# A hybrid decoder layer on one core: halo rows, y splits and one projection step change their places around the output projection

## The chip, the cores and the metric

The kernel runs on one core of a Trainium2 chip. A core has a matrix engine (TensorE, PE in the profile; its weight loads are PEld), a vector engine (VectorE, DVE), a scalar engine (ScalarE, ACT), GpSimd (POOL) and a queue engine that here issues every DMA (SyncE, SP). Each engine works off its own list of instructions in order and waits on semaphores of the others. The metric is device time in microseconds of one execution; the kernel before is given as the median of three.

## The reference, cut to what matters

One layer, float32, 16 meta tokens ahead of 1024 tokens, model width 1024:

```python
xn = rms_norm(h, mix_pre_g)
proj = xn @ w_in                       # z, xbc, dt, q, k, v
y_ssd = ssd_mixer(z, xbc, dt, ...)     # 16 heads, chunks of 128
y_sb = rms_norm(stick_breaking_attention(q, k, v), sb_norm_g)
mix = concat([y_ssd, y_sb]) @ w_out    # 2048 -> 1024
h = h + rms_norm(mix, mix_post_g)
xn = rms_norm(h, ffn_pre_g)
gu = xn @ w_up                         # 2 x 2816 columns
g = causal_dwconv(gu[..., :D_FF], ffn_conv_w, ffn_conv_b)   # 3 taps
f = (gelu(g) * gu[..., D_FF:]) @ w_down
h = h + rms_norm(f, ffn_post_g)
return h[:, N_META:]
```

The convolution of three taps makes token t need the tokens t-1 and t-2. So the last two meta tokens are carried through the mixer and the norm as well, though they are not put out: they are the "halo" below, two rows beside the eight blocks of 128 tokens.

## The kernel before, in words

Every float32 product is made of three passes over rounded parts: an operand x is split into a rounded high part (ScalarE, a copy) and a low part x - high (VectorE or GpSimd, a subtraction), and PE adds high·high, high·low and low·high.

**The attention part.** A loop over eight head pairs p and eight query blocks i. A step makes the scores z (L765), two sigmoids per score tile (kp and bt, L766 and L767, ScalarE), a scan (L773, VectorE), a product (L775, GpSimd), and, some steps later, turns the weights bt by PE transposes (tw, L787), copies them out (th, L789) and multiplies with the values (av, L802, copied out at L805). Score tiles and turned tiles share two PSUM buffers of one tag ("zz"), so a transpose waits until an older score tile is read, and a score tile until an older turned tile is copied. Between these, `fill` gives the projections of q, k and v in half chunks (pj_k and the like, L165), and W_out's first half is loaded and split in eight rows (L887 and L888). "Corner turns" (`edge_turn`, twc, L811, then thc, L814) and `edge_mix` (avc, L822) bring in the keys of block borders once per head pair, at i = 2 and i = 3. At (p, i) = (7, 1) the halo of the first half of W_out begins (`halo_rows`, L916: 64 matmuls of two rows in one PSUM tile, copied out in eight small pieces at L923 and stored by SP), and behind it the first output chain `first` (`ssd_half`, mo, L951, copied out as ma, L963). In this part PE's order is that of the program text; the other engines are ordered by a scheduler. The PSUM tag "mm" has two buffers for pj, halo and mo.

**The second output chain.** A loop t = 1 to 8 over blocks of 128 tokens; from t = 2 on PE, VectorE, ScalarE and GpSimd run in the order of the program text (`manual_schedule`), SP's order is the scheduler's. For a block:

- y (the attention's result, from DRAM) is split: yh (L938, ScalarE) and yl (L939, VectorE for t up to 5, GpSimd after). The buffers of yh and yl hold two blocks.
- mo: two halves of 512 columns, 24 matmuls each (L951); each half is added to the stored first part by VectorE (L1436) in one instruction, which frees the PSUM buffer.
- `after`: square and row sum (L1120, ScalarE), root (L191 and L192, GpSimd), scale and add x (L1123 and L1124, VectorE), square again (L1129), root, scale (L1133, giving oxn). The last two stand in the next step.
- `turn_x2`, two steps later: eight PE transposes (x2tp, L1139) and for t up to 4 two rounded copies, two plain copies (L1145 and L1146, ScalarE) and two subtractions (L1147, VectorE).

The halo goes the same way as a thin block of two rows: `halo_sum` (L1199), `after(0, ...)`, and `turn_x2(0, 2, ...)`. A two-row instruction of 1024 columns lasts as long as one of 128 rows. After the loop come the first feed-forward products (g0a, u0a), then the feed-forward stage to the end.

Names with numbers: x2tp0 is the halo's transpose tile and x2tp3 that of block 3; mo1_5_0 is the first column half of block 5 in the second chain; oxn, jk and mb carry the block too.

Of the kernel before, what the change touches and what calls it, by code (L numbers as in the profile page):

```python
# [9 lines left out]
F32 = mybir.dt.float32  # L10
# [7 lines left out]
P = 128  # L18
# [9 lines left out]
NT = T // P  # L28
# [25 lines left out]
def tile_layer(ctx: ExitStack, tc: tile.TileContext, x, meta, rows, parts,  # L54
               w_z, w_xbc, w_dt, w_q, w_k, w_v, w_out, w_up, w_down, out):
    nc = tc.nc
# [113 lines left out]
    def run(steps, n=None):  # L170
        for _ in steps if n is None else zip(range(n), steps):
            pass
# [280 lines left out]
    with tc.tile_pool(name="ssd", bufs=1, side="right") as sp:  # L453
# [135 lines left out]
        fill = flow([x_flow(0, 0), x_flow(0, 1)], 2)  # L589
# [118 lines left out]
        fill = flow(xz_flow(1), 2)  # L708
# [98 lines left out]
    def edge_turn(p):  # L807
        cb = edges.pop(p)
        tw = psum_tp(f"twc{p}")
        for j in range(2):  # L810
            nc.tensor.transpose(tw[:, j, :], cb[:, j].rearrange("p t c -> p (t c)"), ident)  # L811
        th = ap.tile([P, 2, 4, P], F32, tag="th", name=f"thc{p}", bufs=2).rearrange("p h b c -> p h (b c)")
        for j in range(2):
            nc.vector.tensor_tensor(th[:, j, :256].rearrange("p (t c) -> p t c", c=32),  # L814
                                    tw[:, j, 96:P].unsqueeze(1).to_broadcast([P, NT, 32]), cmask, op=ALU.mult)
        return th
# [95 lines left out]
    def halo_rows(pool, half, y0, w, acc):  # L912
        for k in range(8):
            yield
            for c in range(4):
                mm(acc[32 * c:32 * c + 2, :], y0[:, k, :], w[k][c // 2][:, 512 * (c % 2):512 * (c % 2) + 512].bitcast(F32),  # L916
                   start=k == 0, stop=k == 7)
        for a in (0, 256):
            mh = pool.tile([P, 256], F32, tag="ma", name=f"mh{half}_{a}", bufs=1)
            for c in range(4):  # L920
                b = 512 * (c % 2) + a
                rows_ = slice(32 * c, 32 * c + 2)
                nc.scalar.activation(mh[rows_], acc[rows_, a:a + 256], AF.Copy)  # L923
                nc.sync.dma_start(out=halod[2 * half + c // 2][:, b:b + 256], in_=mh[rows_])
# [3 lines left out]
    def load_y(half, t, yk):  # L928
        nc.sync.dma_start(out=yk, in_=yd1[t - 1] if half else yd[t])
        return yk  # L930

    def split_y(pool, half, t, tags, yk=None, eng=nc.gpsimd):
        nm = f"{half}_{t}"
        if yk is None:
            yk = load_y(half, t, yraw[0](f"yk{nm}"))
        yh = pool.tile([P, 8, P], F32R, tag=tags[0], name=f"yh{nm}", bufs=tags[2])
        yl = pool.tile([P, 8, P], F32R, tag=tags[1], name=f"yl{nm}", bufs=tags[2])
        nc.scalar.activation(yh, yk, AF.Copy)  # L938
        eng.tensor_tensor(yl, yk, yh.bitcast(F32), op=ALU.subtract)  # L939
        return yh, yl  # L940
# [48 lines left out]
    for p in range(8):  # L989
        for i in range(NT):  # L990
            if p == 0 and i == 0:
                run(fill, 1)
            block = block_weights(p, i)
            next(block, None)
            if mix:
                block_mix(*mix.pop(0))
            if p > 0 and i == 3:
                edge_mix(p - 1, edge)
            run(fill, 1 + (i < FILL[p]))
            if first:  # L1000
                run(first, 1)
            run(block)
            if (p, i) == (7, 1):
                halo = halo_rows(ap, 0, y0a, wres, psum_mm("halo0"))
                run(halo, 3)
            ahead = iter(())
            if len(turn) > 2:
                ahead = begin_turn()
            if (p, i) == (7, 1):
                run(halo, 2)  # L1010
            if i < NT - 1:
                run(ahead)
            run(fill, int(p > 0 or i > 3))
            if (p, i) == (7, NT - 1):
                run(first, 1)
            run(ahead)
            if left[0] and wsteps is None:
                wres = []
                wsteps = wout_steps(third_slots(), 0, ssd_g, wres, [])
                y0a = halo_y(ap, 0)  # L1020
            if (p, i) == (6, 3):
                yk = [load_y(0, 1, rp.tile([P, L + 3], F32, tag="rq", name="yk0_1", bufs=3)[:, :D]
                             .rearrange("p (a b) -> p a b", b=P)),
                      load_y(0, 2, rp.tile([P, L], F32R, tag="rk", name="yk0_2", bufs=3).bitcast(F32)[:, :D]
                             .rearrange("p (a b) -> p a b", b=P))]
            if left[1] and not ys1:
                ys1.append(split_y(wp, 0, 1, ("whi", "wlo", WB), yk[0], nc.vector))
            for _ in range(2):
                if wsteps and len(wres) < min(8, 3 * left[0], STAGE.get((p, i), 0)):
                    run(wsteps, 1)  # L1030
            if wsteps and first is None and len(wres) == 8:
                run(wsteps)
                first = ssd_half(wres, ys1)
                run(first, 1)
                ys1.append(split_y(wp, 0, 2, ("whi", "wlo", WB), yk[1], nc.vector))
            elif first:
                run(first, 1)
                run(halo)
            if p == 7 and 2 < i < 6:
                run(meta_steps, 1)  # L1040
            if p == 0 and i == 2:
                token_rstd(r_ssd, ap, "a")
            if p > 0 and i == 2:
                edge = edge_turn(p - 1)
    while turn or mix:
        if mix:
            block_mix(*mix.pop(0))
# [3 lines left out]
    edge = edge_turn(7)  # L1051
# [372 lines left out]
    for t in range(1, NT + 1):  # L1424
        if t == 2:
            order.enter_context(tc.manual_schedule(engines=ORDERED))
        if 1 < t < NT - 1:
            yk = load_y(1, t + 1, yraw[0](f"yk1_{t + 1}"))
        if mts:
            mt = mts.pop(0)  # L1430
        else:
            mt = f1.tile([P, 1032], F32, tag="gr", name=f"mb{t}", bufs=2)[:, :D]
            nc.sync.dma_start(out=mt, in_=mixd[t - 1])

        def ev2(acc, cs, mt=mt, t=t):
            nc.vector.scalar_tensor_tensor(mt[:, cs], acc, r_sb[:, t:t + 1], mt[:, cs], op0=ALU.mult, op1=ALU.add)  # L1436

        if t == 5:
            b22s.append(qp.tile([P, 4, 2 * P], F32, name="b22s", tag="b22s"))
        if t < NT:  # L1440
            xt = wp_f32("wlo", f"xr{t}") if t > 2 else wp.tile([P, D], F32, tag="wraw", name=f"xr{t}")
            nc.sync.dma_start(out=xt, in_=x[(t - 1) * P:t * P, :])
        if t == 7:
            xt8 = qp.tile([P, D], F32, name="xr8", tag="xr8")
            nc.sync.dma_start(out=xt8, in_=x[T - P:, :])
            for jj in range(2):
                load_raw(jj, 0, wp, "wraw", 2)
        steps = out_steps(1, t, wres2, ys.pop(0), ev2)
        run(steps, 2)
        run(norm, 1)  # L1450
        if len(pend) > 1:
            turn = pend.pop(0)()
            run(turn, 2)
            run(norm)
            if t == NT:
                run(steps)
            run(turn)
        run(norm)
        if 1 < t < NT - 1:
            ys.append(split_y(op, 1, t + 1, ("yh", "yl", 2), yk, nc.vector if t < 5 else nc.gpsimd))  # L1460
        if t == 2:
            halo_sum(2)
        elif t == 3:
            halo_sum(3)
            halo_norm = after(0, halo_mt, 2, halo_xt, halo_mo, halo_mo)
            run(halo_norm, 1)
        elif t == 4:
            run(halo_norm)
        if t == 7:
            g0.split_1()  # L1470
            load_raw(0, 1, wp, "wraw", 2)
        elif t == NT:
            g0_pair = pair_w("2g0")
            u0.split_1()
            g0.split_2(g0_pair)
            load_raw(1, 1, wp, "wraw", 2)
        run(steps)
        if t == 6:
            edge_x2()
        if t == NT:  # L1480
            break
        if t == 6:
            ys.append(split_y(op, 1, NT, ("yh", "yl", 2)))
        xn = f1.tile([P, 1032], F32, tag="fa", name=f"oxn{t}")[:, :D]
        junk = psum_fa(f"jk{t}").rearrange("p a b -> p (a b)")
        norm = after(t, mt, P, xt, xn, junk)
        run(norm, 1)
        if t == 7:
            xt = xt8
        run(norm, 2)  # L1490
        pend.append(lambda t=t, xn=xn: turn_x2(t, P, xn, x2_tiles(t)))
        if t == 3:
            run(halo_norm, 2)
        elif t == 4:
            run(turn_x2(0, 2, halo_mo, x2_tiles(0)))
    opool.close()
    tA, tB = ExitStack(), ExitStack()
# [372 lines left out]
```

## Time and profile before

| | us |
|---|---|
| median of three runs (lowest, highest) | 1745.74 (1743.22, 1745.97) |
| the profiled execution, whole | 1741.94 |
| its span, first to last instruction | 1740.0 |
| attention steps with the first output chain, up to | about 945 |
| second output chain, from, to | 968, 1075 |
| feed-forward, from, to | 1075, 1740 |

The profile is of one execution, and every time of an instruction is counted from the start of its span. A row of the timeline gives start, length, engine, line, operation, output and inputs, shapes and count; behind it in brackets the idle time of that engine just before, and whose end released it. The view of waits adds up these idle times by the pair of waiting and releasing line. PE's matmuls overlap: one of 512 columns has a length of 0.39 us, but the next starts 0.23 us after it.

### The profile page before, as it was taken

The page shows a single profiled execution, that of the slowest core. Times are in us where ns is not written, and L with a number is a line of the kernel's source. Part 1 is how long each engine was busy: PE and PEld are TensorE (multiplying, and loading weights), DVE is VectorE, ACT ScalarE, POOL GpSimd, SP SyncE. Part 2 cuts the span into 40 slices and gives each one's busy share as a digit, 9 for nine tenths or more (in the row PEclk, how much of TensorE's full clock was granted, in tenths as well). Part 3 has the DMA queues.
Part 4 walks back from the last instruction along what each step waited for, and adds up shares of the span by engine and source line. Part 5 has one row for each costly group of instructions (what it writes and reads, how often), then busy time and mean ns, then how long its engine had stood idle before and what let it go on. Part 6 is the DMA issues. An engine that isn't in the chain of part 4 may idle for free.

```text
span 1740.0 us, 28052 instructions
## 1 busy us (share of the span) xinstructions
PE 1707.8 (98%) x11230; PEld 1496.6 (86%) x11230; DVE 1121.2 (64%) x1230; ACT 822.9 (47%) x1374; POOL 857.9 (49%) x645
## 2 busy tenths in 40 slices
PE   7999999999999999999999979999999999999998
PEld 6999889888999998998687768999988888887886
DVE  5752964775676677668532457676666666658777
ACT  5423653545566566558553234533333333343544
POOL 4323663686565566555552124487776777400001
PEclk9999999999999999999999999999999999999999
DMA  4233343231011011122215443232332222395335
GB/s 163 63 110 98 98 135 109 65 95 38 26 37 45 30 37 32 31 62 73 82 57 199 165 145 122 67 116 97 105 108 91 92 91 91 108 322 199 104 110 181
DMA packets 90694, 173.88 MB, mean 100 GB/s; under 512 B 10714, under 2 KB 35834, under 8 KB 90564
## 3 DMA queue, kind: packets, MB, share of 16 engines
q1 hardware_dynamic: 90564, 172.10, 31.2%
q8 instruction: 88, 1.44, 0.4%
q14 instruction: 42, 0.34, 0.1%
HBM read 122.33 MB, written 49.73 MB: 99 GB/s over the span
## 4 chain that ended last, share of the span: by engine, by line
PE 89%; issue 3%; DVE 3%; ACT 2%; POOL 2%; DMA 1%; POOLq 0%; DVEq 0%; SPq 0%; ACTq 0%
PE fX L1280 10%; PE dnA L1690 7%; PE fY L1280 6%; PE fA L1280 6%; PE mo L951 6%; PE pj_k L165 5%; PE pj_v L165 5%; PE pj_z L165 5%; PE dnB L1690 5%; PE pj_q L165 5%; PE pj_X L165 5%; PE av L802 4%; PE z L765 3%; PE tw L787 3%; PE pj_B L165 1%
## 5 line engine op out<-in xcount | busy, mean ns | idle before, releaser
L775 POOL TENSOR_TENSOR bt<-bt,kp 128x256 f32<-128x256 f32 (+7 forms) x128 | 213.0, 1683 | 185.5 <-DVE kp L773 135.2
L773 DVE TENSOR_TENSOR_SCAN kp<-kp,hold 128x272 f32<-128x272 f32 (+7 forms) x128 | 183.4, 1473 | 25.3 <-ACT kp L766 15.0
L1223 POOL TENSOR_TENSOR wlo<-wr,whi 128x1024 fp32r<-128x1024 f32 x43 | 107.9, 2518 | 38.4 <-ACT whi L1222 38.4
L1727 POOL TENSOR_TENSOR fms<-fms 128x1 f32<-128x1 f32 x8 | 3.2, 394 | 223.4 <-ACT dh L1612 197.0
L766 ACT ACTIVATE kp<-z 128x288 f32<-128x288 f32 (+6 forms) x112 | 82.6, 737 | 50.9 <-PE z L765 27.5
L1222 ACT ACTIVATE whi<-wr 128x1024 fp32r<-128x1024 f32 x43 | 45.6, 1060 | 111.6 <-PE fX L1280 68.3
L165 PE MATMUL pj_v<-xs,wh_v 128*128 128x400 f32 (+2 forms) x384 | 94.9, 334 | 0.0
L1352 DVE SCALAR_TENSOR_TENSOR ga<-gr,pp,ga 128x1024 f32<-128x1024 f32 x44 | 72.3, 1643 | 34.9 <-ACT ga L1345 34.1
L165 PE MATMUL pj_k<-xs,wh_k 128*128 128x400 f32 (+2 forms) x384 | 94.5, 333 | 0.0
L165 PE MATMUL pj_q<-xs,wh_q 128*128 128x386 f32 (+2 forms) x384 | 93.9, 331 | 0.0
L789 ACT ACTIVATE th<-tw 128x1024 f32<-128x1024 f32 (+2 forms) x96 | 75.6, 816 | 38.5 <-PE tw L787 38.4
L1612 ACT ACTIVATE dh<-ar 128x512 fp32r<-128x512 f32 x77 | 48.5, 630 | 92.7 <-PE dnB L1690 44.7
L165 PE MATMUL pj_X<-xs,wh_X 128*128 128x400 f32 (+2 forms) x384 | 92.0, 327 | 0.2 <-ACT craw_X L211 0.2
L165 PE MATMUL pj_z<-xs,wh_z 128*128 128x386 f32 (+2 forms) x384 | 91.5, 326 | 0.0
L951 PE MATMUL mo<-woa,yh 128*128 128x512 f32 x256 | 84.4, 398 | 2.1 <-ACT ma L963 1.2
L1613 DVE TENSOR_TENSOR dl<-ar,dh 128x512 fp32r<-128x512 f32 x77 | 53.2, 692 | 50.4 <-ACT dh L1612 50.3
L741 DVE CAST qh<-q 128x128 fp32r<-128x128 f32 x64 | 45.7, 715 | 59.7 <-PE z L765 59.4
L767 ACT ACTIVATE bt<-z 128x288 f32<-128x288 f32 (+6 forms) x112 | 82.9, 740 | 0.0
L802 PE MATMUL av<-th,v 128*64 128x128 f32 x1152 | 77.2, 278 | 0.0
L787 PE MATMUL tw<-ident,bt 128*128 128x128 f32 x576 | 75.7, 274 | 0.9 <-ACT bt L767 0.5
L802 PEld LDWEIGHTS av<-th,v 128*64 128x64 f32 x1152 | 61.5, 136 | 13.8 <-issue 11.1
L787 PEld LDWEIGHTS tw<-ident,bt 128*128 128x128 f32 x576 | 65.5, 141 | 7.1 <-issue 3.3
(558 smaller groups left out, 5648.8 us busy)
## 6 DMA issues: line engine op xcount, KB each, us to landing
wr<-in_w_up SPq DMA_DIRECT2D x44, 512.0 KB
fds<-ga SPq DMA_DIRECT2D x44, 256.0 KB
b<-in_w_down SPq DMA_DIRECT2D x44, 256.0 KB
ar<-fds SPq DMA_DIRECT2D x44, 256.0 KB
fda<-ga SPq DMA_DIRECT2D x33, 256.0 KB
ar<-fda SPq DMA_DIRECT2D x33, 256.0 KB
yk<-yd SPq DMA_DIRECT2D x16, 512.0 KB
wor<-in_w_out SPq DMA_DIRECT2D x12, 512.0 KB
```

The costliest lines, as they stand in the source:

```text
L165: mm(acc[:ncol, :n - s], a[:, k, :ncol], xs[c0][:, b, k, s:n], start=(k == 0 and j == 0), stop=(k == KB - 1 and j == 2))
L766: nc.scalar.activation(kp[:, :, a:a + w], z[:, :, :w], AF.Sigmoid, scale=-QSCALE)
L767: nc.scalar.activation(bt[:, :, a:a + w], z[:, :, :w], AF.Sigmoid, scale=QSCALE)
L773: nc.vector.tensor_tensor_scan(kp[:, j][:, ::-1], kp[:, j][:, ::-1], hold[:, L - n:L][:, ::-1], 0.0, op0=ALU.mult, op1=ALU.max)
L775: nc.gpsimd.tensor_tensor(bt[:, j, 0:m], bt[:, j, 0:m], kp[:, j, 1:m + 1], op=ALU.mult)
L787: nc.tensor.transpose(tw[:, j, b, :], bt[:, j, c0:c0 + P], ident)
L789: nc.scalar.activation(th[:, :, :nb, :], tw[:, :, :nb, :], AF.Copy)
L802: mm(av[halves[j], :], v[:, kb, halves[j]], th[:, j, b, :], start=kb == 0, stop=kb == i)
L951: mm(acc, u[:, k, :], v[:, cs], start=(k == 0 and j == 0), stop=(k == 7 and j == 2))
L1223: nc.gpsimd.tensor_tensor(l, raw, h.bitcast(F32), op=ALU.subtract)
L1280: mm(acc[:, c, :nn], u[:, k, :], v[:, k, c0:c0 + nn], start=first and k == 0 and j == 0, stop=k == 3 and j == 2, skip_group_check=not first)
L1690: mm(banks[BANK[n], t], u[:, 0, c], v[:, 1, :], start=(n in (1, 2, 5) and p == 0 and i == 0), stop=(p == NPR - 1 and i == 2), skip_group_c ...
```

## The change

```diff
         for a in (0, 256):
-            mh = pool.tile([P, 256], F32, tag="ma", name=f"mh{half}_{a}", bufs=1)
+            mh = pool.tile([P, 256], F32, tag="ma", name=f"mh{half}_{a}", bufs=2)
...
             ahead = iter(())
+            if (p, i) == (6, 6):
+                run(fill, 1)
             if len(turn) > 2:
                 ahead = begin_turn()
...
-            run(fill, int(p > 0 or i > 3))
+            run(fill, int((p > 0 or i > 3) and (p, i) != (6, 6)))
...
+            if p > 0 and i == 2:
+                edge = edge_turn(p - 1)
             for _ in range(2):
                 if wsteps and len(wres) < min(8, 3 * left[0], STAGE.get((p, i), 0)):
                     run(wsteps, 1)
...
             elif first:
+                run(halo)
                 run(first, 1)
-                run(halo)
...
-            if p > 0 and i == 2:
-                edge = edge_turn(p - 1)
...
-        if 1 < t < NT - 1:
-            yk = load_y(1, t + 1, yraw[0](f"yk1_{t + 1}"))
+        if t == 1:
+            yk = load_y(1, 3, yraw[0]("yk1_3"))
...
         run(steps, 2)
         run(norm, 1)
+        if 1 < t < NT - 1:
+            ys.append(split_y(op, 1, t + 1, ("yh", "yl", 2), yk, nc.vector if t < 5 else nc.gpsimd))
+            yk = load_y(1, t + 2, yraw[0](f"yk1_{t + 2}"))
         if len(pend) > 1:
...
         run(norm)
-        if 1 < t < NT - 1:
-            ys.append(split_y(op, 1, t + 1, ("yh", "yl", 2), yk, nc.vector if t < 5 else nc.gpsimd))
...
         if t == 6:
-            ys.append(split_y(op, 1, NT, ("yh", "yl", 2)))
+            ys.append(split_y(op, 1, NT, ("yh", "yl", 2), yk))
...
-        elif t == 4:
+        elif t == 5:
             run(turn_x2(0, 2, halo_mo, x2_tiles(0)))
```

It does five things. The small halo copies get a second buffer. At step (6, 6) of the attention the second half of a projection chunk goes ahead of a turn. The corner turn goes ahead of W_out's rows in the text of a step, and at (7, 2) the rest of the halo's matmuls ahead of the next piece of the first output chain. In the second chain each y block is split in the middle of a step, ahead of the turn, and loaded a step earlier. And the halo's own transposes go from the end of step 4 to the end of step 5.

Three places show how instructions move. First ScalarE at step (6, 6) (th6_4 are the copies of the turned tiles tw6_4, kh7 the copy of the projection pj_k7, yh0_2 a split of a y block of the first chain, ysc a copy of av, kp6_7 the first sigmoid on the next score tile). Before:

```order
L805 ACTIVATE ysc6_8441<-av6_3_8675 128x128
L789 ACTIVATE th6_4_0_8707<-tw6_4_0_8698 128x1024
L789 ACTIVATE th6_4_1_8712<-tw6_4_1_8709 128x2x128
L938 ACTIVATE yh0_2_9002<-yk0_2_8487 128x1024
L388 ACTIVATE kh7_8088<-pj_k7_784_8685 128x256
L766 ACTIVATE kp6_7_8736<-z6_7_0_8738 128x2x348
```

In the changed kernel:

```order
L805 ACTIVATE ysc6_8441<-av6_3_8675 128x128
L938 ACTIVATE yh0_2_9002<-yk0_2_8487 128x1024
L388 ACTIVATE kh7_8088<-pj_k7_784_8685 128x256
L789 ACTIVATE th6_4_0_8721<-tw6_4_0_8712 128x1024
L789 ACTIVATE th6_4_1_8726<-tw6_4_1_8723 128x2x128
L766 ACTIVATE kp6_7_8736<-z6_7_0_8738 128x2x348
```

The two copies of the turned tiles went behind the y split and the projection's copy, as on PE the ten transposes tw6_4 went behind the twelve matmuls of pj_k7 and now stand directly ahead of the score tile z6_7_0.

Second PE at step (7, 2) (mo0_1_0 and mo0_1_1 are the column halves of block 1 in the first chain, twc6 the corner turn of head pair 6). Before:

```order
L951 MATMUL mo0_1_1_9079<-woa400_8643,yl0_1_8729 128x512
L951 MATMUL mo0_1_1_9079<-woa400_8643,yh0_1_8728 128x512
L916 MATMUL halo0_8945<-woa400_8643,y00_8396 2x512 x8
L916 MATMUL halo0_8945<-woa784_8906,y00_8396 2x512 x8
L811 MATMUL twc6_9126<-ident_69,cb6_8109 128x128 x2
L765 MATMUL z7_3_0_9134<-kh7_8088,qh7_3_9017 128x264 x2
```

In the changed kernel:

```order
L951 MATMUL mo0_1_0_8989<-woa784_8906,yh0_1_8728 128x512
L787 MATMUL tw7_0_0_9074<-ident_69,bt7_0_8837 128x128 x2
L811 MATMUL twc6_9079<-ident_69,cb6_8109 128x128 x2
L916 MATMUL halo0_8945<-woa400_8643,y00_8396 2x512 x8
L916 MATMUL halo0_8945<-woa784_8906,y00_8396 2x512 x8
L951 MATMUL mo0_1_1_9119<-woa0_8406,yh0_1_8728 128x512
L951 MATMUL mo0_1_1_9119<-woa0_8406,yl0_1_8729 128x512
```

The corner turn and the last halo matmuls (x8 is eight matmuls of one form) stand now between mo0_1_0 and mo0_1_1, where nothing stood but tw7_0. At (6, 2), the other place where W_out's rows and a corner turn meet, neither PE's order nor VectorE's is another.

Third ScalarE in the second chain, from the squares of block 4 on. Before:

```order
L1120 ACTIVATE jk4_10567,oss4_10568<-mb4_10481 128x1024
L1129 ACTIVATE jk4_10567,oss24_10577<-mb4_10481 128x1024
L1145 ACTIVATE b11h_10125<-x2tp0_10579 128x4x2
L1146 ACTIVATE xa_10129<-x2tp0_10579 128x4x2
L1145 ACTIVATE b21h_10127<-x2tp0_10579 128x4x2
L1146 ACTIVATE xc_10131<-x2tp0_10579 128x4x2
L1145 ACTIVATE b11h_10125<-x2tp3_10631 128x4x128
L1146 ACTIVATE xa_10129<-x2tp3_10631 128x4x128
L1145 ACTIVATE b21h_10127<-x2tp3_10631 128x4x128
L1146 ACTIVATE xc_10131<-x2tp3_10631 128x4x128
L938 ACTIVATE yh1_6_10647<-yk1_6_10594 128x1024
L1120 ACTIVATE jk5_10678,oss5_10679<-mb5_10596 128x1024
```

In the changed kernel:

```order
L1122 ACTIVATE jk4_10569,oss4_10570<-mb4_10481 128x1024
L1131 ACTIVATE jk4_10569,oss24_10579<-mb4_10481 128x1024
L938 ACTIVATE yh1_6_10616<-yk1_6_10519 128x1024
L1147 ACTIVATE b11h_10125<-x2tp3_10622 128x4x128
L1148 ACTIVATE xa_10129<-x2tp3_10622 128x4x128
L1147 ACTIVATE b21h_10127<-x2tp3_10622 128x4x128
L1148 ACTIVATE xc_10131<-x2tp3_10622 128x4x128
L1122 ACTIVATE jk5_10665,oss5_10666<-mb5_10581 128x1024
L1131 ACTIVATE jk5_10665,oss25_10675<-mb5_10581 128x1024
L1147 ACTIVATE b11h_10125<-x2tp0_10677 128x4x2
L1148 ACTIVATE xa_10129<-x2tp0_10677 128x4x2
```

The split of block 6 went ahead of the four copies of x2tp3, and the halo's four small copies from the front of step 5 to behind its second square. VectorE's yl for blocks 3 to 5 and its halo subtractions moved in the same way; GpSimd's order is the same. On PE the eight transposes x2tp0 went from ahead of mo1_5_0 to ahead of mo1_6_0. On SP the loads of y1_3, y1_6, y1_7 and y1_8 went a few places forward, past loads of x and of the first chain's sums.

## The prediction

> **What bounds the kernel now.** I read the page first, for the busy shares:
>
> ```profile
> PE 1707.8 (98%) x11230; PEld 1496.6 (86%) x11230; DVE 1121.2 (64%) x1230; ACT 822.9 (47%) x1374; POOL 857.9 (49%) x645
> ```
>
> PE is busy 98% of the span, no other engine above 64%. The time is therefore PE's list of instructions plus PE's waits, and a reordering that leaves PE's work alone can only change the waits. So the second view is that of PE's waits (engine, line, whom it waited for; total, times, longest):
>
> ```profile
> PE x2tp L1139 <- DVE mo L1133: 5.9, 1, 5.9
> PE mo L951 <- POOL yl L939: 2.9, 2, 1.5
> PE mo L951 <- DVE yl L939: 1.5, 1, 1.5
> PE mo L951 <- ACT ma L963: 1.2, 2, 0.7
> PE mo L951 <- ACT mh L923: 0.9, 1, 0.9
> PE tw L787 <- ACT bt L767: 0.5, 1, 0.5
> PE tw L787 <- issue: 0.4, 1, 0.4
> PE fX L1280 <- POOL wlo L1223: 0.2, 1, 0.2
> ```
>
> The first three belong to the second output chain: 10.3 us, the most that can be got there by waits alone. The next rows are those of the attention's last steps. The last row is the only wait of PE later than 1075 that this chain can reach: what the chain gains, the end gains. The third view is PE's timeline in the chain, and the windows row of its middle (window, length, PE, PEld, DVE, ACT, POOL, then granted clock, DMA share, GB/s):
>
> ```profile
> 1003.76 0.50 PE L951 MATMUL mo<-wohb,yl 128*128 128x512 f32 x1 [1.49 <-DVE yl L939]
> 1015.23 0.39 PE L951 MATMUL mo<-wolb,yh 128*128 128x512 f32 x1
> 1021.56 0.98 PE L1139 MATMUL x2tp<-ident,mo 2*128 2x2 f32 x8 [5.94 <-DVE mo L1133]
> 1022.47 0.80 PE L951 MATMUL mo<-wohb,yh 128*128 128x512 f32 x1
> 1023.92 0.63 PE L951 MATMUL mo<-wohb,yh 128*128 128x512 f32 x1
> 1024.35 0.63 PE L951 MATMUL mo<-wohb,yl 128*128 128x512 f32 x1
> 1029.76 1.03 PE L1139 MATMUL x2tp<-ident,oxn 128*128 128x128 f32 x8
> 1037.96 0.50 PE L951 MATMUL mo<-wohb,yl 128*128 128x512 f32 x1 [1.46 <-POOL yl L939]
> 1043.33 1.03 PE L1139 MATMUL x2tp<-ident,oxn 128*128 128x128 f32 x8
> 1051.54 0.50 PE L951 MATMUL mo<-wohb,yl 128*128 128x512 f32 x1 [1.48 <-POOL yl L939]
> ...
> 1003.00:1037.00 34.00, 26.80 (x120) 21.68 (x120) 20.53 (x23) 13.29 (x26) 7.86 (x13) 0.90 0.42 139
> ```
>
> The halo's turn at 1021.56 costs more than its 5.94. Behind it the matmuls are 0.43 us apart (1023.92 to 1024.35), and the window's granted clock is 0.90. An undisturbed half from its second matmul on takes 1043.33 - 1037.96 = 5.37, that is 0.23 for each of 23; 24 of them would be 5.6. The half behind the long wait took 1029.76 - 1022.47 = 7.29. So 1.7 us were lost to the clock. With the four waits (5.94, 1.49, 1.46, 1.48) the chain loses 12.1 us. Shorter waits, as that at 1037.96, left the spacing at 0.23.
>
> [...]
>
> **Second chain.** These rows of ScalarE, VectorE and GpSimd carry the sum:
>
> ```profile
> 1002.49 1.22 DVE L939 TENSOR_TENSOR yl<-yk,yh 128x1024 fp32r<-128x1024 f32 x1
> 1013.23 1.06 ACT L1129 ACTIVATE mo<-mb 2x1024 f32<-2x1024 f32 x1 [1.26 <-POOL ms_ff L191]
> 1017.07 1.06 ACT L938 ACTIVATE yh<-yk 128x1024 fp32r<-128x1024 f32 x1
> 1019.01 1.22 DVE L939 TENSOR_TENSOR yl<-yk,yh 128x1024 fp32r<-128x1024 f32 x1
> 1020.15 1.27 DVE L1133 SCALAR_TENSOR_TENSOR mo<-mb,rs_ff,gffn 2x1024 f32<-2x1024 f32 x1
> 1021.34 0.73 DVE L1436 SCALAR_TENSOR_TENSOR mb<-mo,r_sb,mb 128x512 f32<-128x512 f32 x1
> 1026.98 1.03 ACT L1129 ACTIVATE jk<-mb 128x1024 f32<-128x1024 f32 x1 [3.66 <-DVE mb L1124]
> 1033.65 1.06 ACT L938 ACTIVATE yh<-yk 128x1024 fp32r<-128x1024 f32 x1
> 1034.79 3.12 POOL L939 TENSOR_TENSOR yl<-yk,yh 128x1024 fp32r<-128x1024 f32 x1 [5.70 <-ACT yh L938]
> ```
>
> *Step 4.* yl4, which ended 1002.49 + 1.22 = 1003.7, goes ahead of the block's subtractions and is ready before PE asks: the wait of 1.49 is gone, and block 4's product ends near 1014.1 (1015.23 + 0.39 - 1.49).
>
> *Step 5.* The halo's turn no longer stands ahead of it, so 5.94 and the clock loss leave this place. Late next is yl5. VectorE has the same instructions between the sums as before, yl among them, only in another order, so I leave the halo's square at 1013.23. It ends with its read-out near 1014.4; yh5 directly behind it takes 1.0 (to 1015.4), and yl5 1.14 (1019.01 to the next start 1020.15), to 1016.6. PE has block 5's first matmul by 1014.1 and then idles about 2.5. With 5.4 for the first half, 0.8 for the turn of block 3 and about 5.5 for the second half, PE is at 1028.4, and with the halo's turn (0.9, from 1021.56 to 1022.47) at 1029.3. This turn now waits for nothing: its input, the row at 1020.15, is long there.
>
> *Step 6.* The sum at 1021.34, behind the same VectorE work, stays, so the square of block 4 ends near 1028.1 as in its row at 1026.98. yh6 directly behind it: 1029.1, in place of 1033.65 + 1.06. GpSimd's 3.12: 1032.2. PE idles again, 1029.6 to 1032.3, about 2.7. Its second matmul of block 6 starts at 1032.3 against 1037.96: 5.7 earlier.
>
> *Step 7.* Halves and turn as before bring PE to 1044.1; yl7, by the same chain of sum, root, square, yh, yl one block later, ends near 1045.1. So 0.9 of the wait of 1.48 stays, and the matmul of 1051.54 starts at 1045.2: 6.3 earlier. What it gives back follows from the last norm:
>
> ```profile
> 1085.59 1.28 DVE L1133 SCALAR_TENSOR_TENSOR oxn<-mb,rs_ff,gffn 128x1024 f32<-128x1024 f32 x1 [0.45 <-POOL rs_ff L192]
> 1087.42 1.03 PE L1139 MATMUL x2tp<-ident,oxn 128*128 128x128 f32 x8
> ```
>
> The last turn, at 1087.42, has 0.55 of air behind its oxn8 (1085.59 + 1.28). The norms of the last blocks hang on VectorE, where a yh and a yl (1.0 + 1.14 = 2.1) now lie ahead of a turn's subtractions; an estimate is that they gain that much less than PE, 6.3 - 2.1 = 4.2. So 6.3 - 4.2 - 0.55 = 1.6 at most is waited for there. If the last block's norm follows PE, it is 0. I take 0.9. **Sum of the chain: -5.4** (bounds -3.8 by the full payback and 0.9 more of yl's wait, and -12.1, where nothing waits).
>
> **SP's queue.** The loads of y1_7 and y1_8 pass loads of x and of first sums; a load that waits for its buffer then holds these back by 1 or 2 us. VectorE's additions of x wait for roots, not for them: 0, bounds 0 and +1.
>
> **Step (7, 2)**, and the second buffer of the halo copies:
>
> ```profile
> 841.92 0.50 PE L951 MATMUL mo<-woa,yh 128*128 128x512 f32 x1 [0.56 <-ACT ma L963]
> 844.86 3.62 PE L916 MATMUL halo<-woa,y 128*2 128x512 f32 x32
> 853.24 1.56 ACT L923 ACTIVATE mh<-halo 2x256 f32<-2x256 f32 x4
> 854.85 0.50 PE L951 MATMUL mo<-woa,yh 128*128 128x512 f32 x1 [0.88 <-ACT mh L923]
> ```
>
> The halo's 3.62 us of matmuls now stand where PE waited 0.56 for ma, and cover it. The second four copies (853.24) held the PSUM buffer for which the row at 854.85 waited 0.88; with their own buffer and the matmuls some 3 us earlier they end before 850. Both waits go: **-1.4**, bounds -1.4 and 0 (other waits of the same sizes behind the later projection of this block). At the corner turn of (6, 2) neither PE's nor VectorE's list changes: 0.
>
> **Step (6, 6)** is the part that costs:
>
> ```profile
> 808.73 1.07 PE L787 MATMUL tw<-ident,bt 128*128 128x128 f32 x8 [0.40 <-issue]
> 810.32 0.44 PE L787 MATMUL tw<-ident,bt 128*128 128x128 f32 x2 [0.53 <-ACT bt L767]
> 812.12 0.43 PE L765 MATMUL z<-kh,qh 64*128 64x348 f32 x2
> ...
> 810.26 1.36 ACT L789 ACTIVATE th<-tw 128x1024 f32<-128x1024 f32 x2
> 812.11 1.06 ACT L938 ACTIVATE yh<-yk 128x1024 fp32r<-128x1024 f32 x1 [0.49 <-PE pj_k L165]
> ```
>
> With the projection's matmuls ahead of the turn, its waits of 0.40 and 0.53 are covered: -0.93. But the score tile (812.12) came behind some 1.6 us of projection (from the end of the second turn at 810.5 to 812.12), in which ScalarE copied the turned tiles. Now it stands directly behind the turn, and these copies stand behind yh0_2 (1.06) and the projection's copy. PE would be at the score tile by 811.2; ScalarE starts yh near 810.3 and has copied the first turned tile near 812.5. A new wait of about 1.4: **+0.45** net, bounds -0.9 and +0.6 (yh only as late as in its row).
>
> **Sum:** -5.4 - 1.4 + 0.45 = -6.35. The profiled execution was 1741.94 with a span of 1740.0; it would become 1735.6 with a span of 1733.7. The median of the runs is 1745.74, 3.8 above that execution, so by the same difference the median becomes **1739.4**. About 0.2%, 3.5 us, is what can be told from no change here.
>
> **Rivals.** (a) The clock falls again. Two idle gaps of 2.5 and 2.7 lie between the 1.49 that left it alone and the 5.94 that did not, and at the second stand the halo's tiny transposes. At 1.7 a gap: 1741.1 with one, 1742.8 with two. They are nearer to 1.49. 13 in 100.
>
> (b) No new waits: yl5 and yl6 come in time, because ScalarE has an idle microsecond ahead of 1013.23 in which yh5 fits if its order allows. Then up to 12.1 + 1.4 - 0.45 = 13: 1732.7. Against it: yh5 stands behind that square in ScalarE's list. 8 in 100.
>
> (c) PE runs ahead and waits at the end: the norms of blocks 7 and 8 do not come earlier at all, and x2tp of block 8 takes back 5 and more of it: a gain of 0 to 3, about 1744. Against it: these norms hang on PE's sums, which do come earlier. 9 in 100.
>
> (d) Slower: the split, ahead of the turn, delays the copies of the turn and oxn by yh and yl, 1.0 + 1.14 = 2.1 a step, and the chain of norms then sets the pace for four steps (3 to 6): +8.4, less 1.4 of (7, 2), plus 0.45: +7.4, 1753. It decides where a norm has less than 2 us of air. Against it: yl5 (1019.01) stood between the subtractions and the sum at 1021.34 already, so the sum has the same work ahead of it. 13 in 100.
>
> **How the numbers follow.** The forecast has 57 in 100, with a range of its own from 1736.5 to 1742. Faster by over 0.2% (below 1742.2): nearly all of it, (a) for the most part, (b): 0.71. Within 0.2%: two gaps in (a), (c), a little of the forecast: 0.16. Slower: (d), 0.13. The range leaves out (d) and the larger part of (b): 1735 to 1745.5.
>
> **What would show it.** Right: no wait of x2tp for the halo's mo; a granted clock of 1.0 between 1003 and 1037, with matmuls 0.23 apart behind every wait; waits of mo for VectorE's yl of about 2.5 near 1014, and for GpSimd's yl of 2.7 near 1030 and 0.9 near 1044; at (7, 2) no waits for ma and mh; near 811 a new wait of z for ScalarE's th of about 1.4. Wrong: spacings of 0.43 in the chain; a wait of x2tp for oxn of blocks 2 to 5; a wait of the last x2tp above 1.6; feed-forward waits that were not there.

## The result

| | us | ratio to before (95% interval) |
|---|---|---|
| before, median of 4 runs (lowest, highest) | 1745.51 (1743.22, 1745.97) | |
| changed, median of 4 runs | 1737.07 (1736.02, 1739.22) | 0.9953 (0.9937 to 0.9969) |
| changed, a second time, median of 6 runs | 1737.08 (1734.39, 1739.18) | 0.9958 (0.9945 to 0.9972) |
| span of the profiled execution, before and changed | 1740.0 and 1734.1 | |

The change makes the kernel faster by 0.4 to 0.5%, some 7 to 8 us; the forecast, 1739.4 of 1745.74, is a ratio of 0.9964 and lies in both intervals. Between the two profiled executions the difference is 5.9 us, and that can be followed instruction by instruction.

First the view of PE's waits in the changed kernel (lines behind the edits have moved by 2):

```profile
PE z L765 <- ACT th L789: 1.9, 1, 1.9
PE mo L951 <- POOL yl L939: 1.4, 2, 0.9
PE x2tp L1141 <- DVE oxn L1135: 1.0, 1, 1.0
PE mo L951 <- ACT yh L938: 0.8, 1, 0.8
PE mo L951 <- DVE yl L939: 0.8, 1, 0.8
PE mo L951 <- ACT ma L963: 0.6, 1, 0.6
```

The wait of 5.9 for the halo's mo is gone, as are the wait for mh, one of the two for ma and both for bt. What stands in their place is shorter, but for the first row, which is new. The timeline of PE in the second chain and the window that showed 0.90 before:

```profile
1002.79 0.39 PE L951 MATMUL mo<-wohb,yl 128*128 128x512 f32 x1
1015.31 0.50 PE L951 MATMUL mo<-wohb,yh 128*128 128x512 f32 x1 [0.80 <-ACT yh L938]
1016.57 0.50 PE L951 MATMUL mo<-wohb,yl 128*128 128x512 f32 x1 [0.76 <-DVE yl L939]
1019.50 0.63 PE L951 MATMUL mo<-wohb,yl 128*128 128x512 f32 x1
1019.93 0.63 PE L951 MATMUL mo<-wolb,yh 128*128 128x512 f32 x1
1029.98 0.65 PE L1141 MATMUL x2tp<-ident,mo 2*128 2x2 f32 x8
1031.51 0.50 PE L951 MATMUL mo<-wohb,yl 128*128 128x512 f32 x1 [0.45 <-POOL yl L939]
1044.49 0.50 PE L951 MATMUL mo<-wohb,yl 128*128 128x512 f32 x1 [0.92 <-POOL yl L939]
1081.64 1.06 PE L1141 MATMUL x2tp<-ident,oxn 128*128 128x128 f32 x8 [1.02 <-DVE oxn L1135]
...
1003.00:1037.00 34.00, 31.99 (x145) 25.43 (x144) 20.40 (x22) 13.94 (x24) 8.85 (x15) 0.95 0.45 143
```

Row by row against the timeline shown of before: the matmul of 1003.76 now starts at 1002.79 without a wait, that of 1037.96 at 1031.51, that of 1051.54 at 1044.49, and the last turn at 1081.64 in place of 1087.42. The clock still falls (0.43 between 1019.50 and 1019.93), and the window's clock is 0.95.

To add this up, take the start of the same PE instruction in both profiles; the difference is a shift, and what a stretch adds to the shift is what it costs or gains. The shift is +2.0 already at 806, ahead of all edits that move PE's instructions; step (6, 6) adds 0.6 (to 836), step (7, 2) takes 1.8 (836 to 870), the chain takes 6.4 (985 to 1089), and at the end it is -5.7. The two early microseconds are two falls of the clock that, of these two executions, only the changed kernel's has; the windows rows are:

```profile
54.00:58.00 4.00, 4.00 (x16) 4.00 (x17) 4.00 (x4) 1.94 (x3) 2.38 (x1) 0.67 0.44 130
416.70:420.50 3.80, 3.80 (x23) 3.22 (x24) 1.93 (x6) 2.29 (x5) 1.83 (x1) 0.56 0.00 0
```

PE is busy through both (4.00 of 4.00, 3.80 of 3.80), so no wait explains them; before had 1.00 at both places. Without them the profiles would differ by 7.9, close to the medians' 8.4.

### The profile page after: what moved, and what is told of

Read it like the earlier page. It is cut to its first block, busy times and chain, and to the rows that moved or that the text cites. A ratio compares the mean times of both kernels' runs of the same rounds, so it can differ in the third digit from the quotient of the medians.

```text
span 1734.1 us, 28054 instructions
## 1 busy us (share of the span) xinstructions
PE 1710.1 (99%) x11230; PEld 1499.7 (86%) x11230; DVE 1115.5 (64%) x1230; ACT 823.1 (47%) x1374; POOL 857.0 (49%) x645
## 5 line engine op out<-in xcount | busy, mean ns | idle before, releaser
L165 PEld LDWEIGHTS pj_v<-xs,wh_v 128*128 128x128 f32 x384 | 65.4, 190 | 5.9 <-issue 5.7
```

The costliest lines, as they stand in the source:

```text
L165: mm(acc[:ncol, :n - s], a[:, k, :ncol], xs[c0][:, b, k, s:n], start=(k == 0 and j == 0), stop=(k == KB - 1 and j == 2))
```

## The experiments

All are the kernel before or the changed one with the edits named; none leaves work out. The table has the three stretches of each profile as shifts against before (us, minus is faster), and the ratio by time.

| kernel | step (6, 6), 806 to 836 | step (7, 2), 836 to 870 | chain, 985 to 1089 | ratio (95% interval) |
|---|---|---|---|---|
| changed | +0.6 | -1.8 | -6.4 | 0.9953 (0.9937 to 0.9969) |
| changed, again | +2.0 | -1.8 | -6.5 | 0.9958 (0.9945 to 0.9972) |
| halo's turn moved, alone | +1.1 | +0.1 | -2.6 | 0.9983 (0.9973 to 0.9992) |
| y splits moved, alone | +0.1 | +0.1 | -2.7 | 0.9974 (0.9965 to 0.9984) |
| both, alone | +2.9 | +0.1 | -6.4 | 0.9957 (0.9944 to 0.9969) |
| halo edits alone | +0.6 | -1.8 | +1.1 | 0.9988 (0.9979 to 0.9997) |
| halo buffer alone | +2.6 | -1.0 | +0.8 | one run, 1745.16 |
| halo order alone | +2.7 | -1.8 | +0.2 | one run, 1744.77 |
| step (6, 6) alone | +0.5 | +0.1 | +0.4 | 1.0002 (0.9993 to 1.0011) |
| changed without (6, 6) | +2.7 | -1.8 | -6.5 | 0.9949 (0.9937 to 0.9960) |
| early splits, without (6, 6) | +2.9 | -1.8 | -7.7 | 0.9948 (0.9936 to 0.9960) |
| early splits, moved sums, without (6, 6) | +2.8 | -1.8 | -7.5 | 0.9948 (0.9936 to 0.9960) |
| early splits, moved sums, with (6, 6) | +3.1 | -1.8 | -7.1 | 0.9957 (0.9943 to 0.9970) |

**Parts of the chain.** The halo's turn moved, alone:

```diff
-        elif t == 4:
+        elif t == 5:
             run(turn_x2(0, 2, halo_mo, x2_tiles(0)))
```

> The kernel before with one edit: the halo's transposes go to the end of step 5. Theory: the wait of 5.94 for the halo's mo goes, but yl5 (its end was 1020.2) takes its place: PE waits about 4.6 for VectorE's yl ahead of block 5's second matmul, and behind so long a gap the clock falls again, so that matmuls stand 0.43 apart for some 3 us. PE is then 2.5 to 3.5 us earlier at the end of the chain: 1742 to 1743, ratio about 0.998. Rival (the wait was the whole loss): 5.94 and 1.7 of clock are won, 1738, ratio 0.9956.

Its PE timeline has two waits at block 5:

```profile
1020.46 0.50 PE L951 MATMUL mo<-wohb,yh 128*128 128x512 f32 x1 [2.57 <-ACT yh L938]
1022.57 0.80 PE L951 MATMUL mo<-wohb,yl 128*128 128x512 f32 x1 [1.60 <-DVE yl L939]
```

The 5.94 became 2.57 + 1.60, and the clock fell behind it (the matmul at 1022.57 has a length of 0.80, as the one at 1022.47 in before, where the matmuls stood 0.43 apart). The gain, 2.6 in the profile and 0.17% by time, is the theory's; the rival's 0.9956 lies outside the interval.

The splits and loads of y moved, alone (the edits of the loop at `load_y`, `split_y` and block 8 in the diff above):

> The kernel before with one edit: each y block is split ahead of the turn and loaded a step earlier; the halo's transposes stay at the end of step 4. Theory: the input of the halo's turn stays at 1021.4, so PE, 1.5 earlier, waits longer for it, 7 in place of 5.94, and the clock falls as before; yl6 and yl7 come in time, as PE is later than in the full change: their waits of 1.46 and 1.48 go. Gain 3 us: 1742.5, ratio 0.998. Rival (each wait removed is won): 4.4 us, ratio 0.9975; rival (nothing is won without the halo's move, the long wait swallows it): 0 to 1 us.

```profile
PE x2tp L1139 <- DVE mo L1133: 7.0, 1, 7.0
```

As expected, the wait of 5.94 grew to 7.0, as PE came earlier to an input that did not, and the waits for yl are gone. By time, 0.9974 fits both 0.998 and 0.9975, so that adding up the removed waits is not refuted by it; the profile's 2.7 is nearer to the first. Nothing won at all is refuted. But the 2.7 holds a longer fall of the clock. The trace's record of the granted clock has half speed at the halo's wait and behind it for 10.24 us in this profile, and for 6.83 in before; the windows rows of 1013 to 1034 are, for before, this kernel and the halo edits alone:

```profile
1013.00:1034.00 21.00, 15.06 (x67) 12.23 (x66) 10.84 (x15) 9.24 (x20) 3.14 (x8) 0.84 0.44 150
1013.00:1034.00 21.00, 14.03 (x55) 11.19 (x54) 12.10 (x15) 8.91 (x18) 5.49 (x9) 0.76 0.55 174
1013.00:1034.00 21.00, 15.06 (x62) 12.31 (x62) 11.30 (x14) 7.83 (x16) 2.10 (x5) 0.76 0.40 126
```

The halo edits alone, and the halo buffer alone, leave the chain's instructions as before and have the 10.24 too: they are 1.1 and 0.8 longer in the chain, where the halo order and step (6, 6) alone, with 6.83, are 0.2 and 0.4 longer.

Both together, without the attention part:

> The kernel before with both edits of the second chain, without those of the attention part. Theory: the gain of the chain as the profile of the changed kernel has it, 6.5 us: 1739, ratio 0.9963, with two waits of about 0.8 at block 5, 0.5 at block 6, 0.9 at block 7 and 1.0 at the last turn. Whether the clock falls behind block 5's two short waits tells whether that fall belongs to them. Rival (most of the gain is from the attention part, whose 1.9 the profile shows): under 4 us.

The chain gains 6.4 in the profile, with the same waits as in the changed kernel. That is 1.1 more than 2.6 + 2.7, which the longer fall in the second profile can explain. In the waits of the chain the two edits take away 2.5 and 3.1 apart, and 6.4 together, 0.8 more. By time they add up: 0.17% and 0.26% apart, 0.43% together. So that the pair is worth more than its parts is not shown; what is shown is that with the splits alone the long wait took back 1.0 of the 1.5 won ahead of it.

**The halo edits.** The three together, then the buffer and the order apart (the order with the corner turn ahead of W_out's rows, as in the diff of the change):

```diff
-            mh = pool.tile([P, 256], F32, tag="ma", name=f"mh{half}_{a}", bufs=1)
+            mh = pool.tile([P, 256], F32, tag="ma", name=f"mh{half}_{a}", bufs=2)
```

```diff
             elif first:
+                run(halo)
                 run(first, 1)
-                run(halo)
```

> The kernel before with the edits at the corner turns and the halo's matmuls and the second buffer of the halo copies. Theory: the waits for ma (0.56) and mh (0.88) go, with the slow restart behind each, 1.9 us as in the changed kernel, and the second chain is as before: 1743.6, ratio 0.9989. Rival (the second chain's norms, not PE, set its pace, and it waits longer): 0, ratio 1.000.

> The kernel before with the second buffer of the halo copies alone. Theory: the second four copies no longer wait for the first four's way out, so mo's wait of 0.88 for mh goes, and the wait of 0.56 for ma stays; 1 us. Rival (the copies are late because the halo's matmuls are, and ScalarE's kp, bt and ysc stand between): the wait for mh stays.

> The kernel before with the corner turn ahead of W_out's rows and the rest of the halo's matmuls ahead of the next piece of the first chain, but one buffer for the halo copies. Theory: the matmuls stand where the wait for ma of 0.56 was and cover it, and the copies run some 3 us earlier, so both waits go without the second buffer: 1.4 to 1.9 us. Rival (the second buffer is needed): mo waits for mh as before.

The three together measured 0.9988, as expected. In its profile the buffer alone takes away the wait for mh and leaves that of 0.6 for ma: -1.0. The order alone takes away both: -1.8, as much as all three. So the second buffer adds nothing once the matmuls stand earlier; that the order would do without it was the theory of this run, and it holds.

**Step (6, 6).**

```diff
+            if (p, i) == (6, 6):
+                run(fill, 1)
...
-            run(fill, int(p > 0 or i > 3))
+            run(fill, int((p > 0 or i > 3) and (p, i) != (6, 6)))
```

> The kernel before with the edit of step (6, 6) alone. Theory: a wait of z for th of 1.9 in place of the two for bt, with a turn that no late load can delay; 0 to +0.6 us, ratio 1.000. Rival (a hedge that pays mostly): -1 us, 0.9994. An interval of some 1 us either way will not tell these apart by time; the waits of the profile will show what the turn waits for.

> The changed kernel with step (6, 6) put back: the projection behind the turn again. Theory: the new wait of 1.86 for th goes and the old waits for bt come back. They were 0.93 where ScalarE's W_out row did not wait for its load, and 2.1 and 2.6 in two profiles where it did (1.06 and 2.11 late): so 0.9 us faster than the changed kernel where the load is in time, 0.3 to 0.7 slower where it is late; in the median within 1 us of the changed kernel's 0.9953. Rival (the edit is a plain loss, as the sum of the prediction had it): faster by 0.5 to 1 in every execution, 0.9949. Rival (it is worth more than the profile shows): slower by 1 or more, 0.996.

By time the edit is nothing: 1.0002, and 0.9949 without it against 0.9953 and 0.9958 with it. The profiles say why the sum of the prediction does not decide it. In the profile of before the turn at 808.73 waited 0.40. In the changed kernel without this edit it waited 2.06, and on ScalarE a split of a W_out row (L887) ahead of the sigmoids had waited for its load:

```profile
812.03 1.21 PE L787 MATMUL tw<-ident,bt 128*128 128x128 f32 x8 [2.06 <-issue]
...
807.92 1.16 ACT L887 ACTIVATE woa<-wor,pp 128x1024 fp32r<-128x1024 f32 x1 [1.54 <-DMA wor<-in_w_out]
```

Behind that row stand the sigmoids that free the score tile's buffer, so the turn is late by what the load is late: in the ten profiles with the old order its first wait is the lateness plus 0.4 to 0.5 (lateness and wait are 0 and 0.40, 0.20 and 0.71, 1.06 and 1.58, 1.54 and 2.06, 2.11 and 2.62). These ten have stretches of 0 to +2.9 here, on average 1.8; the four with the new order +0.5 to +3.1, on average 1.6. The new order's wait for th of 1.8 to 1.9 is there each time; a late load reached it too, as a wait of 0.53 for bt in the kernel of the table's last row.

The other part is the clock. Behind these waits it was at half for 3.41 us in six of the ten, and these have +2.6 to +2.9; the other four have 0 to +1.1. Of the four with the new order it was in two, with +2.0 and +3.1; the other two have +0.5 and +0.6. The load's lateness and the clock are a matter of the execution, and larger than what the edit moves.

**Other places for the splits.** In the changed kernel without step (6, 6), each block from 4 on is split a whole step earlier than in the kernel before, at the end of a step, where ScalarE and VectorE wait for the norm, and every yl is VectorE's:

```diff
+        if 1 < t < NT - 1:
+            ys.append(split_y(op, 1, t + 2, ("yh", "yl", 2), yk, nc.vector))
+            if t < NT - 2:
+                yk = load_y(1, t + 3, yraw[0](f"yk1_{t + 3}"))
         xn = f1.tile([P, 1032], F32, tag="fa", name=f"oxn{t}")[:, :D]
```

> The changed kernel with step (6, 6) put back and another place of the splits: block t + 2 is split at the end of step t, ahead of the block's norm, all on VectorE, and loaded a step before. Theory: the waits of the second chain for yh and yl (0.80, 0.76, 0.45, 0.92) are all gone, the wait of the last turn for oxn8 of 1.0 stays or grows to 2, and with no gap at block 5 the granted clock stays at 1.0 there: 2 to 4 us faster than the changed kernel, 1733.5 to 1735.5. Rival (the splits then delay the norms by 1.0 + 1.14 each, and turns wait for oxn of blocks 3 to 6): as the changed kernel or slower. Rival on the clock (it falls there without a gap as well): matmuls 0.43 apart for 3 us near 1015.

All waits for yh and yl are gone, and the window has a clock of 1.00. In their place PE waits for VectorE's sum (it frees the PSUM buffer) and longer for the last norm, beside three new waits of 0.3 to 0.5; these are the two and, from VectorE's timeline, the reason for the first:

```profile
PE mo L951 <- DVE mb L1436: 1.7, 2, 1.2
PE x2tp L1139 <- DVE oxn L1133: 1.5, 1, 1.5
...
1015.54 1.27 DVE L1123 SCALAR_TENSOR_TENSOR mb<-mb,rs_mo,gpost 2x1024 f32<-2x1024 f32 x1
1016.84 1.21 DVE L1124 TENSOR_TENSOR mb<-mb,xr 2x1024 f32<-2x1024 f32 x1
1017.98 0.73 DVE L1436 SCALAR_TENSOR_TENSOR mb<-mo,r_sb,mb 128x512 f32<-128x512 f32 x1
...
1003.00:1037.00 34.00, 32.03 (x152) 25.92 (x151) 22.87 (x24) 15.75 (x27) 6.32 (x14) 1.00 0.46 147
```

The halo's two rows keep VectorE for 2.4 us ahead of the sum (1.27 and 1.21 for two rows, where the same two lines took 1.28 and 1.23 for block 4's 128 rows just before). The chain gains 1.3 more than the changed kernel, less than the 2 to 4 expected. So the sums were moved:

```diff
+        if t == 4:
+            run(halo_norm, 2)
...
+        if 3 < t < NT - 1:
+            run(steps)
         run(norm)
...
-        if t == 3:
-            run(halo_norm, 2)
-        elif t == 5:
+        if t == 5:
```

> The early splits with three further moves on VectorE: in steps 4 to 6 a block's second sum stands ahead of the norm's scale of the block before, and the halo's additions and its second square stand behind the first sum of block 4. Theory: the waits of mo for VectorE's sum (1.21 and 0.45 with the early splits) go, block 4's norm is some 2 us earlier, and what is left is the last turn's wait, 1.5 or less: 1.5 to 3 us faster than with the early splits alone, 1732 to 1733.7, ratio 0.994. Rival (the last block's norm sets the end): the last turn's wait grows by what is won before, no change from the early splits, 0.9948.

```profile
PE x2tp L1139 <- DVE oxn L1133: 3.1, 2, 1.6
```

The waits for the sum are gone, and the same time is now waited for oxn, at two turns: the rival is right. Once y is early, PE waits for the norms on VectorE, and this other order of the same instructions does not win more.

> The kernel of the sums with step (6, 6) as in the changed kernel. Theory: within 1 us of the kernel without it, either way; its profile has the wait of 1.9 for th, and the other the waits for bt of 0.9 to 2.6 by how late the load of a W_out row lands. Rival (a plain loss): 0.6 to 1 slower.

0.9957 against 0.9948 without (6, 6), with intervals that overlap; the chain of this profile is also 0.4 worse, though the edit stands far ahead of it. The three kernels without (6, 6) have 0.9948 or 0.9949, the best measured; that they beat the changed kernel is likely but not shown, since their intervals reach up to 0.9960.

**The changed kernel once more:**

> The changed kernel once more, for its interval and a second profile. Theory: the waits of the chain repeat to 0.1 us (0.80 and 0.76, the last turn 1.0) as does the new one of 1.86 for th, and the clock falls again behind block 5's two waits, while the falls near 55 and 417, which have no wait ahead of them, come and go. Ratio 0.995 to 0.996. Rival (all three falls belong to the program): the same three again.

The two falls at 55 and 417 were not there, as expected (two others were, at 814 and 879); the waits of 0.79 and 0.76 were. But the clock did not fall behind them; it fell behind a longer wait for yl6 (from this profile's timeline, and its windows row of the chain's middle):

```profile
1017.42 0.50 PE L951 MATMUL mo<-wohb,yl 128*128 128x512 f32 x1 [0.76 <-DVE yl L939]
1032.32 0.53 PE L951 MATMUL mo<-wohb,yl 128*128 128x512 f32 x1 [1.93 <-POOL yl L939]
1033.93 0.63 PE L951 MATMUL mo<-wolb,yh 128*128 128x512 f32 x1
1034.36 0.63 PE L951 MATMUL mo<-wohb,yh 128*128 128x512 f32 x1
...
1003.00:1037.00 34.00, 30.49 (x138) 24.19 (x136) 20.87 (x22) 13.93 (x24) 8.38 (x15) 0.95 0.43 141
```

In the first profile the fall at block 5 made PE late enough for yl6 to be waited for 0.45 alone. The chain's gain is the same, 6.4 and 6.5: most of the 1.7 of the fall at block 5 came off the wait for yl6, which is 0.45 in the first profile and 1.93 in the second.

## Why the prediction was right

- **PE is the bound, and its waits are the time.** Right. What the waits gave is what the end moved by, but for falls of the clock. That the total came within 2.3 us of the forecast is in part luck: the new gaps were put too long, and a fall of the clock in the chain was put at nothing; the two errors have opposite signs.
- **Chain, -5.4.** The mechanism was right, the size 1.0 short: -6.4, and -6.5 again. The mis-sized terms are the gaps at blocks 5 and 6. Block 5's, put at 2.5, was 0.80 + 0.76. I had left the halo's square at 1013.23 although PE's frame would move: it started at 1013.16 in an execution in which PE came to the chain 0.7 later, so the chain on VectorE and ScalarE did gain, by 0.75, which fits yl4's new place ahead of its subtractions. Block 6's gap, put at 2.7, was 0.45 or 1.93. There yl6 took 2.38 and not 3.12:

```profile
1029.07 2.38 POOL L939 TENSOR_TENSOR yl<-yk,yh 128x1024 fp32r<-128x1024 f32 x1
```

- **What is left behind it.** yl7's wait was put at 0.9 and is 0.92, the last turn's at 0.9 and is 1.02. (In the second profile they are nothing and 0.7, behind the longer wait for yl6.) That turn is the one place where the gain is given back, as the prediction had it.
- **SP's queue, 0.** No wait of PE or VectorE for a moved load is in the profile.
- **Step (7, 2), -1.4.** It was -1.8. Both waits are gone; 0.2 of the difference is in the restarts, as the second matmul behind each of the two waits came 0.33 or 0.34 after the first in before, where 0.23 is usual. The second buffer had no part in it.
- **Step (6, 6), +0.45.** The wait of 1.4 for th was 1.86, and the stretch cost 0.6 in the first profile. But the price of the old order, which the prediction took from one profile as 0.93, is 0.9 to 2.6 of waits by when a W_out row lands, and in six of the ten profiles with that order, 3.41 us of the clock at half. The edit's effect by time is 0, to 0.1% either way; this is the step whose row was not representative.
- **Rival (a), the clock.** It happened, in one of the two gaps in each profile. In the first it did not cost its 1.7, since it shortened the wait behind it by 1.5 (1.93 to 0.45). A granted clock of 1.0 in the window was wrong, and the spacings of 0.43, named as a sign of being wrong, were there. The lengths it reasoned from, 1.49 and 5.94, do not tell the cases apart: the clock fell behind 0.80 + 0.76 in the first profile and not behind 0.79 + 0.76 in the second, where it fell behind 1.93, and with the moved sums and (6, 6) it did not fall behind 2.00.
- **Rivals (b), (c), (d).** (b) needs waits to vanish, which the early splits did: the chain then gained 7.7, not the 12 of the sum, as the norms took over. (c) is there with 1.0 of its 5. (d), the norms delayed by 2.1 a step, does not show: no turn of blocks 2 to 5 waits for oxn in the changed kernel.

## What to carry to other kernels

Where one engine is busy all the time, look for pairs of waits on one path: with the short ones alone removed, the long one grew from 5.94 to 7.0; with the long one alone removed, 4.2 of other waits took its place; without both, 1.56 was left there. Before you compare such parts by single profiles, see how long the clock was down in each. A wait measured in one profile is a sample: before paying for its removal, look in other profiles at the same place for what it hangs on, here a load and the clock. And two edits that remove the same wait (a buffer and an order) should be tried apart, since one may do.

## What the runs showed of the hardware

The clock fell also without any wait ahead of it. In 6 of the 14 profiles it fell near 417, behind this row of 18 matmuls of a single column, which count as busy:

```profile
414.72 2.07 PE L445 MATMUL pta<-ones,sq 128*2 128x1 f32 x18
```

In 3 of the 14 it fell near 55, behind 18 matmuls of 16 columns (2.09 us), and in 7 near 880, behind 16 matmuls of four columns (1.94 us). Each of these falls cost 1.1 to 1.6, and the same instruction list did or did not have it: of the changed kernel's two profiles the first has the falls near 55 and 417, the second the one near 880.

Behind waits the same holds. Block 5's two waits in the changed kernel's first profile, 0.80 and 0.76, had the clock at half behind them for 3.41 us (0.50 from 1018 to 1021). In its second profile they were 0.79 and 0.76, and the clock stayed at 1.00 from 1015 to 1022; behind the 1.93 for yl6 it was 0.58 from 1032 to 1036. In the kernel with the moved sums and (6, 6) it stayed at 1.00 behind a wait of 2.00:

```profile
1024.62 1.06 PE L1141 MATMUL x2tp<-ident,oxn 128*128 128x128 f32 x8 [2.00 <-DVE oxn L1135]
...
1003.00:1037.00 34.00, 31.07 (x150) 25.41 (x149) 22.73 (x24) 15.54 (x27) 7.43 (x13) 1.00 0.44 145
```

So in these profiles neither the instruction list nor the length of a wait alone decides whether the clock falls; what does is not shown.

These falls and the loads' landing are part of the spread between runs: at 985, ahead of the second chain, the shifts of the 13 other profiles against before are between -2.4 and +5.5, far more than the edits ahead of it explain. The unprofiled runs bear this out for the clock, since the record has a mean granted clock for each: of 53 runs of the kernel before in the three later sets, the 12 at 0.994 or less took 1746.6 on average, the 29 at 0.996 took 1744.1, and the three at 0.997 took 1741.8. One stretch of 3.41 us at half speed is 1.7 us of full speed in some 1740, 0.001 of the mean clock. Whether this is also why medians move by 2 us between sets of runs (1745.5, 1745.0, 1744.6 and 1743.9 for the kernel before) is not shown, as the later sets ran on different chips.
